# Weight and operand sums of a Strassen value projection moved to VectorE, its two half results kept apart in DRAM

## The chip, the cores and the metric

One core of one Trainium2 chip. The metric is the device time of the core for one execution of the whole program, in microseconds (us). The core has TensorE (PE in the profile, with its weight loads as PEld), VectorE (DVE), ScalarE (ACT), GpSimd (POOL) and SyncE (SP), which issues nearly all of the DMAs here.

## The reference

Two layers over x of 512 tokens by 2048 features, all in float32. The even layer comes first (sliding-window attention and a gated recurrence) and is not touched. The odd layer is the one that matters:

```python
def odd_layer(x, ln, w_in, w_out):
    h = rmsnorm(x, ln).astype(x.dtype)
    cq, ck, cv, cg = jnp.split(h @ w_in, 4, axis=-1)      # each 512 x 2048
    ...
    oc = stick_breaking_attention(heads(cq), heads(ck), heads(cv))   # 16 heads of 128
    y = (oc * jax.nn.silu(cg.astype(jnp.float32))).astype(x.dtype) @ w_out
    return x + y
```

The change concerns `cv`, the values: 512 tokens times a 2048 by 2048 weight.

## The kernel before

**Exact products.** Every float32 operand of a matmul is carried as two parts: ScalarE copies it into `hi` with rounding to fp32r (L169), VectorE takes `lo = raw - hi` (L170), and each product is three matmuls, hi·hi, lo·hi and hi·lo. Weight pieces (`raw`, 512 KB) are loaded by SP, split into `hi` and `lo` of a pool `w` with three buffers each, and taken by TensorE in a fixed order. `take()` hands out one piece and `pump()` splits up to three ahead, so VectorE can be at most about three takes ahead of TensorE. TensorE's own order is written out by hand; the other queues are ordered by a scheduler, each runs its instructions strictly in that order.

**The value projection.** The 2048 by 2048 weight is cut into four blocks of 1024 by 1024, by rows (`kh`, a half of the features) and columns (`g`, eight heads). `V_ORDER` is (g,kh) = (0,0), (1,0), (1,1), (0,1): block 0 to block 3. Each block is done by Strassen's scheme (Winograd's form) with seven products of quarters in place of eight. A product is two takes of 12 matmuls each: 2 chunks of 128 rows, 2 token halves, 3 parts. The seven products of four blocks are 672 matmuls of 128x512.

Strassen needs sums ahead of the products. *Weight sums*, function `quarter_sum`: t3 = "22"-"12" (L229), t1 = "12"-"11" (L233), t2 = t3+"11" (L237), t4 = "21"-t2 (L241), each in four pieces 128x512, so 16 per block and 64 in all, on GpSimd. The last three overwrite their inputs, so t2 has to wait until "11" has been split. `block_ahead` loads the quarters of the next block (tiles `x`, 19 buffers, and `raw`) and takes t3 and t1 early. *Operand sums*, function `operand_pair`: the two input chunks are read back from DRAM (`x1`), scaled on ScalarE (L872), and combined by four 128x256 steps: L874 and L875 on GpSimd, L876 and L877 on VectorE; then each is split. There are four pairs for each kh, made at the places in `OPERANDS_AT`.

**Results.** A product ends in two PSUM banks (128x512 each). For each result it belongs to, the first product is copied by ScalarE (L1044), a later one is added by VectorE (L1047), both marked urgent. In the kernel before, the two halves kh of a column group g go into the same tiles `halves[g]`: group 1 keeps its tiles from block 1 to block 2; group 0 is written to the DRAM tensor `vdr` after block 0, fetched again during block 2 (`fetch_half`, L1019, eight DMAs), and added into by block 3. So blocks 2 and 3 only add, by VectorE. When a group of four heads begins, SP fetches four tiles of `vdr` (L1078), which are scaled by the token norm and split (L1000, L1001).

**Around it.** Ahead of block 0 stands the even layer's output projection (L827, L850, `finish_even` at L894 to L900), with a running sum of squares on GpSimd (L407). Behind block 3 follow the 16 heads: three projections each, and the attention of the head before it, fed in between them.

Of the kernel before, what the change touches and what calls it, by code (L numbers as in the profile page):

```python
# [9 lines left out]
F32 = mybir.dt.float32  # L10
# [4 lines left out]
ALU = mybir.AluOpType  # L15
# [4 lines left out]
P = 128  # L20
D = 2048
S = 512
NC = D // P
NB = S // P
# [82 lines left out]
def trunk(ctx, tc, xt, w, lnT, lbT, gnT, qkn, sink, cs, amask, bmask, eye, cmask, out):  # L107
    nc = tc.nc
# [9 lines left out]
    dr = ctx.enter_context(tc.tile_pool(name="dr", bufs=1, space=DRAM))  # L118
    V, A, G, T = nc.vector, nc.scalar, nc.gpsimd, nc.tensor
    cnt = [0]  # L120

    def U(dt=F32, shape=(P, S)):
        cnt[0] += 1
        return u.tile(list(shape), dt, tag="u", name=f"u{cnt[0]}")
# [66 lines left out]
    for item in order:  # L191
        n = len(chunk_pieces(item))
# [29 lines left out]
    def quarter_sum(blk, name, i):  # L222

        r = quarters[blk]
        if (name, i) in r:
            return
        if name == "t3":
            r["t3", i] = X()
            G.tensor_tensor(out=r["t3", i], in0=r["22", i], in1=r["12", i], op=ALU.subtract)  # L229
        elif name == "t1":  # L230
            quarter_sum(blk, "t3", i)
            r["t1", i] = r["12", i]
            G.tensor_tensor(out=r["12", i], in0=r["12", i], in1=r["11", i], op=ALU.subtract)  # L233
        elif name == "t2":
            quarter_sum(blk, "t1", i)
            r["t2", i] = r["11", i]
            G.tensor_tensor(out=r["11", i], in0=r["t3", i], in1=r["11", i], op=ALU.add)  # L237
        else:
            quarter_sum(blk, "t2", i)
            r["t4", i] = r["21", i]  # L240
            G.tensor_tensor(out=r["21", i], in0=r["21", i], in1=r["11", i], op=ALU.subtract)  # L241

    def block_ahead(blk, m):

# [223 lines left out]
    for tt, o in ((tq, 0), (tk, 2)):  # L468
        for j in range(2):
            V.tensor_tensor(out=tt[:, j], in0=cst[:, j],  # L470
                            in1=nrm[:, o + j:o + j + 1, :].to_broadcast([P, NB, A_HD]), op=ALU.mult)
# [194 lines left out]
    for i in range(2):  # L666
        t = U(I32, [P, 4, P])
# [137 lines left out]
    for grp in range(2):  # L805
        v = evac_nat(proj_n(h, pp, 512), nat0, 512)
        for hd in range(4 * grp, 4 * grp + 4):
            f, k = forget(proj_t(h), hd)
# [58 lines left out]
    def operand_pair(kh, i):  # L867


        a, b = (sources.pop(c) for c in (8 * kh + i, 8 * kh + 4 + i))  # L870
        for t, c in ((a, 8 * kh + i), (b, 8 * kh + 4 + i)):
            A.activation(out=t, in_=t, func=AF.Copy, scale=ln[:, NC + c:NC + c + 1])  # L872
        a1, a2, b1, b2 = a[:, :256], a[:, 256:], b[:, :256], b[:, 256:]
        G.tensor_tensor(out=b2, in0=a2, in1=b2, op=ALU.add)  # L874
        G.tensor_tensor(out=a2, in0=a1, in1=a2, op=ALU.subtract)  # L875
        V.tensor_tensor(out=a1, in0=b2, in1=a1, op=ALU.subtract)  # L876
        V.tensor_tensor(out=b1, in0=b1, in1=a1, op=ALU.subtract)  # L877
        ops[kh, i] = []
        for t in (a, b):
            hi, lo = U(F32R), U(F32R)  # L880
            split(t, hi, lo)
            ops[kh, i].append((hi, lo))
# [121 lines left out]

    vdr = dr.tile([P, NB, D], F32, tag="vdr", name="vdr")
    halves = {0: {}, 1: {}}
    OPERANDS_AT = {(0, 0): ((0, 1),), (0, 1): ((0, 2), (0, 3)),
                   (1, 5): ((1, 0),), (1, 6): ((1, 1),), (2, 0): ((1, 2),), (2, 1): ((1, 3),)}  # L1010
    operand_loads(0, (2, 3))

    def fetch_half(g):

        for key in ("11", "21", "12", "22"):
            for t in range(2):
                tb, cb = t + 2 * (key[0] == "2"), 2 * g + (key[1] == "2")
                halves[g][key, t] = U()
                nc.sync.dma_start(out=halves[g][key, t], in_=vdr[:, tb, cb * S:(cb + 1) * S])  # L1019

    for blk, (g, kh) in enumerate(V_ORDER):
        res = halves[g]
        banks = {}
        for n, (name, _, pair, new, results) in enumerate(PRODUCTS[blk % 2]):
            if new:
                banks[pair] = [bank(pa if pair == 2 else pp) for _ in range(2)]
            ps = banks[pair]
            for j in range(2):
                hi, lo = take()
                for i in (2 * j, 2 * j + 1):  # L1030
                    a, b = (x[:, (i % 2) * S:(i % 2 + 1) * S] for x in (hi, lo))
                    xh, xl = block_op(kh, name, i)
                    for t in range(2):
                        k = slice(t * P, (t + 1) * P)
                        mm(ps[t], xh[:, k], a, bool(new) and not i, False)
                        mm(ps[t], xl[:, k], a, False, False)
                        mm(ps[t], xh[:, k], b, False, i == 3)
            left = [r for p in PRODUCTS[blk % 2][n + 1:] for r in p[4]]
            for t in range(2):
                for to in results:  # L1040
                    if (to, t) not in res:
                        res[to, t] = U()
                        with urgent():
                            A.activation(out=res[to, t], in_=ps[t], func=AF.Copy)  # L1044
                    else:
                        with urgent():
                            V.tensor_tensor(out=res[to, t], in0=ps[t], in1=res[to, t], op=ALU.add)  # L1047
                    if to not in left and blk != 1:
                        tb, cb = t + 2 * (to[0] == "2"), 2 * g + (to[1] == "2")
                        nc.sync.dma_start(out=vdr[:, tb, cb * S:(cb + 1) * S], in_=res[to, t])  # L1050
            if (blk, n) == (1, 4):
                operand_loads(1)
            for kh_, i in OPERANDS_AT.get((blk, n), ()):
                operand_pair(kh_, i)
            if blk == 2 and n == 4:
                fetch_half(0)

    for grp in range(4):
        for hd in range(4 * grp, 4 * grp + 4):
            ps = proj_t(h2)  # L1060
            if hd == 0:
                bc1, nat1 = token_rstd(acc2, 1)
            q = U()
            with urgent():
                V.scalar_tensor_tensor(out=q, in0=ps, scalar=float(P) ** -0.5, in1=bc1, op0=ALU.mult, op1=ALU.mult)
            q = split_u(q) + (q,)
            ps = proj_t(h2)
            k = U()
            with urgent():
                V.tensor_tensor(out=k, in0=ps, in1=bc1, op=ALU.mult)  # L1070
            k = split_u(k) + (k,)
            if hd == C_HEADS - 1:
                yy = [load_y(c) for c in range(3)]
            g = gate(proj_t(h2), bc1)
            if hd == 4 * grp:
                v = [U() for _ in range(NB)]
                for t in range(NB):
                    nc.sync.dma_start(out=v[t], in_=vdr[:, t, grp * S:(grp + 1) * S])  # L1078
                v[:3] = [split_u(x, nat1[:, t:t + 1]) for t, x in enumerate(v[:3])]
                A.activation(out=v[3], in_=v[3], func=AF.Copy, scale=nat1[:, 3:4])  # L1080
            later(attn_c(hd, q, k, g, v))
# [71 lines left out]
```

## Time and profile before

| | |
|---|---|
| time, three runs | 1840.41, 1842.22, 1842.20 us, median 1842.2 us |
| the profiled execution | 1840.83 us, of which 1839.0 us are its span |
| TensorE busy | 1806.1 us (98%), 8706 matmuls |
| VectorE busy | 1131.6 us (62%) |
| ScalarE busy | 824.5 us (45%) |
| GpSimd busy | 216.4 us (12%) |
| the value projection | from 869.6 to 1054.6 us of the span |

TensorE's busy time counts an instruction from its start to its modelled end, and the matmuls overlap, so a stretch that is fully busy need not be at its best rate; the distance between starts tells that. In a timeline the bracket behind an instruction is the idle time of its engine just before it, and what ended it. [...]

### The profile page before, as it was taken

Reading aid. Unit: us, or ns where it says so; the run is one execution under the profiler, and the core shown is the slowest. Engines: PE = TensorE matmul, PEld = TensorE weight load, DVE = VectorE, ACT = ScalarE, POOL = GpSimd, SP = SyncE. Lnnn points to the kernel's source line nnn. Section 1 sums busy time; section 2 is a strip of 40 time slices with the busy share of each in tenths; the row PEclk is TensorE's granted clock in tenths of the full one; section 3 lists DMA queues with packets and bytes.
Section 4 is the critical chain, followed back from the end, with each engine's and each line's share of the span. In section 5 each row is a group of like instructions: output and inputs, shape, how many; then the busy total and the mean of one; then the engine's idle time right before and its main releaser. Section 6 shows DMA issues by size and latency. Waiting matters only on the chain.

```text
span 1839.0 us, 22928 instructions
## 1 busy us (share of the span) xinstructions
PE 1806.1 (98%) x8706; PEld 1500.0 (82%) x8706; DVE 1131.6 (62%) x1679; ACT 824.5 (45%) x1392; POOL 216.4 (12%) x164
## 2 busy tenths in 40 slices
PE   9999999999999999999788999999999999999999
PEld 6988888888888888888666888888888888888887
DVE  7485777866556676446889845556555565556334
ACT  6455646644244453234553444445444444444211
POOL 5012211200000000126575200000000000000000
PEclk9999999999999999999999999999999999999999
DMA  6222232222222235633443332232223223235424
GB/s 231 92 82 91 81 111 84 83 87 78 75 77 85 77 125 201 208 135 138 150 144 136 121 128 91 93 113 88 95 88 111 98 83 116 90 118 173 164 80 155
DMA packets 80318, 210.32 MB, mean 114 GB/s; under 512 B 9424, under 2 KB 9936, under 8 KB 80208
## 3 DMA queue, kind: packets, MB, share of 16 engines
q1 hardware_dynamic: 77904, 204.67, 32.8%
q10 hardware_dynamic: 2304, 4.20, 0.7%
q8 instruction: 68, 1.11, 0.2%
q14 instruction: 42, 0.34, 0.1%
HBM read 185.76 MB, written 23.07 MB: 114 GB/s over the span
## 4 chain that ended last, share of the span: by engine, by line
PE 91%; DVE 3%; DMA 2%; issue 2%; POOL 1%; ACT 1%; SPq 0%; POOLq 0%; DVEq 0%; ACTq 0%
PE b L166 89%; DVE blo L170 1%; PE b L968 1%; DMA u<-in_w 1%; PE b L621 1%; DVE u L170 1%; DMA raw<-in_w 0%; DVE lo L170 0%; DMA ident<-in_eye 0%; POOL x L241 0%; DVE u L1047 0%; POOL u L407 0%; DMA u<-x 0%; DVE u L876 0%; PE b L552 0%
## 5 line engine op out<-in xcount | busy, mean ns | idle before, releaser
L166 PE MATMUL b<-u,hi 128*128 128x512 f32 x3584 | 1119.3, 393 | 0.0
L166 PEld LDWEIGHTS b<-u,hi 128*128 128x128 f32 x3584 | 663.3, 188 | 132.2
L166 PE MATMUL b<-u,lo 128*128 128x512 f32 x1792 | 698.8, 390 | 1.0 <-DVE lo L170 1.0
L169 ACT ACTIVATE hi<-raw 128x1024 fp32r<-128x1024 f32 (+2 forms) x266 | 269.9, 1015 | 652.8 <-PE b L166 599.7
L170 DVE TENSOR_TENSOR lo<-raw,hi 128x1024 fp32r<-128x1024 f32 (+2 forms) x266 | 313.0, 1177 | 224.3 <-ACT hi L169 209.1
L166 PEld LDWEIGHTS b<-u,lo 128*128 128x128 f32 x1792 | 336.3, 188 | 72.7 <-DVE lo L170 1.4
L166 PE MATMUL b<-hi,u 128*128 128x512 f32 (+1 forms) x640 | 185.1, 374 | 2.8 <-ACT u L446 1.9
L166 PE MATMUL b<-bhi,u 128*128 128x512 f32 x448 | 141.0, 396 | 0.4 <-DVE u L1047 0.4
L166 PEld LDWEIGHTS b<-hi,u 128*128 128x128 f32 x640 | 113.9, 189 | 23.5 <-ACT u L446 2.8
L166 PEld LDWEIGHTS b<-u,u 128*128 128x128 f32 (+2 forms) x928 | 115.7, 176 | 14.9 <-issue 3.5
L166 PE MATMUL b<-u,u 128*128 128x128 f32 (+5 forms) x928 | 126.7, 280 | 0.0
L166 PE MATMUL b<-lo,u 128*128 128x512 f32 (+1 forms) x320 | 118.2, 369 | 0.3 <-DVE lo L170 0.2
L166 PE MATMUL b<-blo,u 128*128 128x512 f32 x224 | 90.9, 406 | 23.0 <-DVE blo L170 22.9
L166 PEld LDWEIGHTS b<-bhi,u 128*128 128x128 f32 x448 | 85.8, 192 | 18.6 <-ACT bhi L169 0.8
L170 DVE TENSOR_TENSOR blo<-x,bhi 128x512 fp32r<-128x512 f32 x80 | 83.7, 1088 | 11.2 <-ACT bhi L169 10.9
L391 DVE TENSOR_TENSOR u<-b,bc 128x512 f32<-128x512 f32 x40 | 27.6, 689 | 79.9 <-PE b L166 79.8
L229 POOL TENSOR_TENSOR x<-x,x 128x512 f32<-128x512 f32 x16 | 24.8, 1553 | 437.4 <-ACT u L169 402.4
L166 PEld LDWEIGHTS b<-blo,u 128*128 128x128 f32 x224 | 43.0, 192 | 39.1 <-DVE blo L170 30.6
L170 DVE TENSOR_TENSOR u<-u,u 128x512 fp32r<-128x512 f32 (+1 forms) x82 | 63.9, 784 | 17.7 <-ACT u L169 17.7
L169 ACT ACTIVATE bhi<-x 128x512 fp32r<-128x512 f32 x80 | 47.2, 624 | 55.5 <-PE b L166 37.1
L166 PEld LDWEIGHTS b<-lo,u 128*128 128x128 f32 x320 | 60.3, 189 | 11.2 <-DVE lo L170 1.1
L170 DVE TENSOR_TENSOR x<-x,x 128x512 fp32r<-128x512 f32 (+2 forms) x56 | 32.4, 579 | 58.3 <-ACT x L169 58.3
(174 smaller groups left out, 1667.7 us busy)
## 6 DMA issues: line engine op xcount, KB each, us to landing
raw<-in_w SPq DMA_DIRECT2D x234, 512.0 KB, 3.2
x<-in_w SPq DMA_DIRECT2D x48, 256.0 KB, 3.1
raw<-in_w SPq DMA_DIRECT2D x24, 384.0 KB, 3.0
ydr<-x SPq DMA_DIRECT2D x32, 256.0 KB, 3.1
u<-ydr SPq DMA_DIRECT2D x32, 256.0 KB, 3.7
u<-x SPq DMA_DIRECT2D x32, 256.0 KB, 4.6
vdr<-u SPq DMA_DIRECT2D x24, 256.0 KB, 2.7
u<-vdr SPq DMA_DIRECT2D x24, 256.0 KB, 4.5
```

Source lines behind the costliest of these rows:

```text
L166: T.matmul(o, l, r, start=start, stop=stop, skip_group_check=True)
L169: A.activation(out=hi, in_=src, func=AF.Copy)
L170: V.tensor_tensor(out=lo, in0=src, in1=hi.bitcast(F32), op=ALU.subtract)
L229: G.tensor_tensor(out=r["t3", i], in0=r["22", i], in1=r["12", i], op=ALU.subtract)
L391: V.tensor_tensor(out=g, in0=ps, in1=bc, op=ALU.mult)
L621: T.transpose(out=pt[:, (2 * i + z) * P:(2 * i + z + 1) * P], in_=probs[p][b][:, z, n * P:(n + 1) * P], identity=ident)
L968: T.transpose(out=o[:, (qb - kb) * P:(qb - kb + 1) * P], in_=zs[qb][:, kb * P:(kb + 1) * P], identity=ident)
```

## The change

The 64 weight sums and the 16 first operand steps (L874, L875) are given to VectorE. The tiles that carried a half result from one block to another are gone: each block starts its own results (so ScalarE makes 32 first copies where it made 16, and VectorE 28 additions where it made 44) and writes them to one of two DRAM tensors, `vdr0` for kh 0 and `vdr1` for kh 1, 32 writes where there were 24. `fetch_half` and its eight reads are gone. When a head group begins, it fetches eight tiles in place of four, and VectorE adds them in pairs (four more 128x512 additions for each of the four groups). Everything else, TensorE's order included, is as before.

```diff
         if name == "t3":
             r["t3", i] = X()
-            G.tensor_tensor(out=r["t3", i], in0=r["22", i], in1=r["12", i], op=ALU.subtract)
+            V.tensor_tensor(out=r["t3", i], in0=r["22", i], in1=r["12", i], op=ALU.subtract)
...
-            G.tensor_tensor(out=r["12", i], in0=r["12", i], in1=r["11", i], op=ALU.subtract)
+            V.tensor_tensor(out=r["12", i], in0=r["12", i], in1=r["11", i], op=ALU.subtract)
...
-            G.tensor_tensor(out=r["11", i], in0=r["t3", i], in1=r["11", i], op=ALU.add)
+            V.tensor_tensor(out=r["11", i], in0=r["t3", i], in1=r["11", i], op=ALU.add)
...
-            G.tensor_tensor(out=r["21", i], in0=r["21", i], in1=r["11", i], op=ALU.subtract)
+            V.tensor_tensor(out=r["21", i], in0=r["21", i], in1=r["11", i], op=ALU.subtract)
...
-        G.tensor_tensor(out=b2, in0=a2, in1=b2, op=ALU.add)
-        G.tensor_tensor(out=a2, in0=a1, in1=a2, op=ALU.subtract)
+        V.tensor_tensor(out=b2, in0=a2, in1=b2, op=ALU.add)
+        V.tensor_tensor(out=a2, in0=a1, in1=a2, op=ALU.subtract)
...
-    vdr = dr.tile([P, NB, D], F32, tag="vdr", name="vdr")
-    halves = {0: {}, 1: {}}
+    vdr = [dr.tile([P, NB, D], F32, tag=f"vdr{i}", name=f"vdr{i}") for i in range(2)]
...
-        res = halves[g]
+        res = {}
...
-                    if to not in left and blk != 1:
+                    if to not in left:
...
-                        nc.sync.dma_start(out=vdr[:, tb, cb * S:(cb + 1) * S], in_=res[to, t])
+                        nc.sync.dma_start(out=vdr[kh][:, tb, cb * S:(cb + 1) * S], in_=res[to, t])
...
-            if blk == 2 and n == 4:
-                fetch_half(0)
...
-                v = [U() for _ in range(NB)]
+                v = []
                 for t in range(NB):
-                    nc.sync.dma_start(out=v[t], in_=vdr[:, t, grp * S:(grp + 1) * S])
+                    parts = U(), U()
+                    for kh in range(2):
+                        nc.sync.dma_start(out=parts[kh], in_=vdr[kh][:, t, grp * S:(grp + 1) * S])
+                    V.tensor_tensor(out=parts[0], in0=parts[0], in1=parts[1], op=ALU.add)
+                    v.append(parts[0])
```

The scheduler makes new queues of this. Three places matter, all on VectorE. In the rows, `blo<-x,bhi` is a `lo` part of a weight piece for a take, `u` are operands or results, `b` PSUM banks.

**Place 1, block 0, around the end of its second product.** Before, VectorE makes the parts of the third product's second take (blo_7452), adds the second product's banks (L1047), and finishes the operand pairs (L876, L877) that GpSimd has begun:

```order
L170 TENSOR_TENSOR blo_7452<-x_7232,bhi_7451 128x512
L170 TENSOR_TENSOR blo_7452<-x_7234,bhi_7451 128x512
L1047 TENSOR_TENSOR u_7409<-b_7427,u_7409 128x512
L1047 TENSOR_TENSOR u_7411<-b_7428,u_7411 128x512
L876 TENSOR_TENSOR u_7363<-u_7365,u_7363 128x256
L877 TENSOR_TENSOR u_7365<-u_7365,u_7363 128x256
L876 TENSOR_TENSOR u_7367<-u_7369,u_7367 128x256
L170 TENSOR_TENSOR blo_7508<-raw_7224,bhi_7507 128x1024
```

GpSimd's queue before, at the same place, from the last weight sums of block 0 (L241, t4) to the operand steps that VectorE's L876 needs:

```order
L241 TENSOR_TENSOR x_7232<-x_7232,raw_7226 128x512
L241 TENSOR_TENSOR x_7234<-x_7234,raw_7226 128x512
L229 TENSOR_TENSOR x_7597<-x_7589,x_7591 128x512
L233 TENSOR_TENSOR x_7591<-x_7591,raw_7543 128x512
L229 TENSOR_TENSOR x_7600<-x_7593,x_7595 128x512
L874 TENSOR_TENSOR u_7365<-u_7363,u_7365 128x256
L233 TENSOR_TENSOR x_7595<-x_7595,raw_7543 128x512
L875 TENSOR_TENSOR u_7363<-u_7363 128x256
```

VectorE now:

```order
L170 TENSOR_TENSOR blo_7453<-x_7232,bhi_7452 128x512
L874 TENSOR_TENSOR u_7366<-u_7364,u_7366 128x256
L1038 TENSOR_TENSOR u_7410<-b_7428,u_7410 128x512
L1038 TENSOR_TENSOR u_7412<-b_7429,u_7412 128x512
L170 TENSOR_TENSOR blo_7453<-x_7234,bhi_7452 128x512
L875 TENSOR_TENSOR u_7364<-u_7364 128x256
L874 TENSOR_TENSOR u_7370<-u_7368,u_7370 128x256
L876 TENSOR_TENSOR u_7364<-u_7366,u_7364 128x256
L875 TENSOR_TENSOR u_7368<-u_7368 128x256
L877 TENSOR_TENSOR u_7366<-u_7366,u_7364 128x256
L876 TENSOR_TENSOR u_7368<-u_7370,u_7368 128x256
L170 TENSOR_TENSOR blo_7509<-raw_7224,bhi_7508 128x1024
```

All steps of the operand pairs stand in one queue now, and the sums for the next block (L229, L233), which stood ahead of them on GpSimd, come later on VectorE.

**Place 2, block 2, its second product and the parts for the third (t4).** VectorE before, from the second product's parts to the third's (blo_8166):

```order
L170 TENSOR_TENSOR blo_8130<-x_7933,bhi_8129 128x512
L170 TENSOR_TENSOR blo_8130<-x_7935,bhi_8129 128x512
L170 TENSOR_TENSOR u_8156<-u_7965,u_8155 128x512
L1047 TENSOR_TENSOR u_7783<-b_8109,u_7783 128x512
L1047 TENSOR_TENSOR u_7785<-b_8110,u_7785 128x512
L170 TENSOR_TENSOR u_8160<-u_7967,u_8159 128x512
L170 TENSOR_TENSOR blo_8166<-x_7911,bhi_8165 128x512
L170 TENSOR_TENSOR blo_8166<-x_7913,bhi_8165 128x512
```

VectorE now, the last twelve rows up to the first half of the same parts (blo_8177):

```order
L237 TENSOR_TENSOR raw_7870<-x_7988,raw_7870 128x512
L875 TENSOR_TENSOR u_7970<-u_7970 128x256
L241 TENSOR_TENSOR x_7914<-x_7914,raw_7870 128x512
L876 TENSOR_TENSOR u_7970<-u_7972,u_7970 128x256
L237 TENSOR_TENSOR raw_7870<-x_7991,raw_7870 128x512
L877 TENSOR_TENSOR u_7972<-u_7972,u_7970 128x256
L170 TENSOR_TENSOR u_8167<-u_7970,u_8166 128x512
L241 TENSOR_TENSOR x_7916<-x_7916,raw_7870 128x512
L1038 TENSOR_TENSOR u_8156<-b_8174,u_8156 128x512
L1038 TENSOR_TENSOR u_8158<-b_8175,u_8158 128x512
L170 TENSOR_TENSOR u_8171<-u_7972,u_8170 128x512
L170 TENSOR_TENSOR blo_8177<-x_7914,bhi_8176 128x512
```

Weight sums t2 and t4 and whole operand pairs now stand in VectorE's queue ahead of the parts that TensorE takes next.

**Place 3, the first head group.** VectorE before, from the gate of head 0 (L391) on:

```order
L391 TENSOR_TENSOR u_8981<-b_8920,bc_8822 128x512
L170 TENSOR_TENSOR lo_9015<-raw_9012,hi_9014 128x1024
L396 SCALAR_TENSOR_TENSOR u_8983<-u_8981,u_8983 128x512
L398 TENSOR_TENSOR u_8981<-u_8981,u_8983 128x512
L1001 SCALAR_TENSOR_TENSOR u_8999<-u_8990,nat_8823,u_8998 128x512
L947 SCALAR_TENSOR_TENSOR x_9046<-b_9024,x_9046 128x512
```

VectorE now:

```order
L391 TENSOR_TENSOR u_8990<-b_8929,bc_8831 128x512
L170 TENSOR_TENSOR lo_9036<-raw_9033,hi_9035 128x1024
L396 SCALAR_TENSOR_TENSOR u_8992<-u_8990,u_8992 128x512
L1070 TENSOR_TENSOR u_8999<-u_8999,u_9000 128x512
L398 TENSOR_TENSOR u_8990<-u_8990,u_8992 128x512
L947 SCALAR_TENSOR_TENSOR x_9067<-b_9045,x_9067 128x512
L1070 TENSOR_TENSOR u_9004<-u_9004,u_9005 128x512
```

The four additions L1070 wait for two DMAs each, and stand among the rows of the attention and ahead of the next `lo`.

## Rows read from the trace of the kernel before

**Rows 1.** Stretches of the span: PE, PEld, DVE, ACT, POOL busy us (instructions), clock, DMA share, GB/s.
```profile
740.00:860.00 120.00, 120.00 (x531) 99.41 (x530) 57.46 (x62) 40.78 (x54) 33.36 (x20) 1.00 0.48 168
860.00:900.00 40.00, 30.39 (x122) 22.86 (x121) 33.95 (x35) 21.63 (x37) 30.00 (x23) 0.94 0.26 89
900.00:940.00 40.00, 40.00 (x172) 32.93 (x172) 31.74 (x35) 21.64 (x37) 18.33 (x12) 0.97 0.48 159
940.00:1000.00 60.00, 46.20 (x183) 34.24 (x182) 54.85 (x57) 27.05 (x44) 40.78 (x29) 0.97 0.39 134
1000.00:1060.00 60.00, 60.00 (x266) 49.72 (x265) 50.18 (x59) 23.61 (x35) 19.43 (x12) 1.00 0.45 151
1060.00:1600.00 540.00, 540.00 (x2552) 450.32 (x2552) 298.68 (x395) 253.38 (x400) 0.00 (x0) 1.00 0.29 99
```

**Rows 2.** TensorE's waits, 860 to 1060: total us, times, longest.
```profile
PE b L166 <- DVE blo L170: 22.9, 13, 5.4
```

**Rows 3.** TensorE's timeline: start, us, what; block 0's start, longest stall, steady rate, end.
```profile
869.55 0.61 PE L166 MATMUL b<-bhi,u 128*128 128x512 f32 x2
...
897.88 0.79 PE L166 MATMUL b<-blo,u 128*128 128x512 f32 x1 [5.38 <-DVE blo L170]
...
905.11 0.62 PE L166 MATMUL b<-bhi,u 128*128 128x512 f32 x2
...
905.79 0.62 PE L166 MATMUL b<-bhi,u 128*128 128x512 f32 x2
...
1054.37 0.39 PE L166 MATMUL b<-blo,u 128*128 128x512 f32 x1
```

**Rows 4.** TensorE alone, short stretches: us, busy (instructions), clock, DMA share, GB/s.
```profile
898.00:902.00 4.00, 4.00 (x10) 0.50 0.65 213
...
994.00:998.00 4.00, 4.00 (x12) 0.57 0.88 290
```

**Rows 5.** Timeline: four GpSimd sums in a row, and VectorE beside them.
```profile
969.10 7.05 POOL L237 TENSOR_TENSOR raw<-x,raw 128x512 f32<-128x512 f32 x4 [3.63 <-DVE blo L170]
...
971.52 1.78 DVE L170 TENSOR_TENSOR blo<-x,bhi 128x512 fp32r<-128x512 f32 x1
973.22 1.78 DVE L170 TENSOR_TENSOR u<-u,u 128x512 fp32r<-128x512 f32 x1
```

**Rows 6.** Timeline of VectorE while GpSimd stands still.
```profile
868.42 0.43 DVE L876 TENSOR_TENSOR u<-u,u 128x256 f32<-128x256 f32 x1 [2.69 <-POOL u L875]
868.88 0.42 DVE L877 TENSOR_TENSOR u<-u,u 128x256 f32<-128x256 f32 x1
...
884.89 0.68 DVE L170 TENSOR_TENSOR blo<-x,bhi 128x512 fp32r<-128x512 f32 x1
885.49 0.68 DVE L170 TENSOR_TENSOR u<-u,u 128x512 fp32r<-128x512 f32 x1
...
898.35 0.41 DVE L877 TENSOR_TENSOR u<-u,u 128x256 f32<-128x256 f32 x1
898.68 1.21 DVE L170 TENSOR_TENSOR blo<-raw,bhi 128x1024 fp32r<-128x1024 f32 x1
899.82 0.68 DVE L170 TENSOR_TENSOR u<-u,u 128x512 fp32r<-128x512 f32 x1
```

**Rows 7.** GpSimd's first sums (t3), 740 to 1060: count, busy us, mean ns, idle before, releasers.
```profile
L229 POOL TENSOR_TENSOR x<-x,x 128x512 f32<-128x512 f32 x16 | 24.8, 1553 | 437.4 <-ACT u L169 402.4 <-DMA x<-in_w 22.5 <-DVE blo L170 12.4
```

**Rows 8.** VectorE, block 0: the wait for an operand step of GpSimd.
```profile
894.56 0.93 DVE L876 TENSOR_TENSOR u<-u,u 128x256 f32<-128x256 f32 x1 [2.58 <-POOL u L875]
```

**Rows 9.** GpSimd's timeline: a sum that waits for its load.
```profile
1000.86 1.29 POOL L229 TENSOR_TENSOR x<-x,x 128x512 f32<-128x512 f32 x1 [8.67 <-DMA x<-in_w]
```

**Rows 10.** The head group's fetch: SP's issue, VectorE behind it, time to landing.
```profile
1086.36 2.06 SPq L1078 DMA_DIRECT2D u<-vdr  x4
...
1098.60 1.22 DVE L170 TENSOR_TENSOR lo<-raw,hi 128x1024 fp32r<-128x1024 f32 x1
...
DMA to landing us min/median/max: 3.7/4.5/4.9
```

More of the change, by code (lines that the diff above doesn't have):

```diff
@@ L1011, in trunk @@
     operand_loads(0, (2, 3))
[L1013 to L1019, printed above, removed]
     for blk, (g, kh) in enumerate(V_ORDER):
-        res = halves[g]
+        res = {}
         banks = {}
```

## The prediction

> **What bounds the kernel now.** I read the stretches first, then TensorE's waits, then its timeline. TensorE is busy without a gap from 740 to 860 and from 1060 to 1600, but only 30.4 of 40 us from 860 to 900 and 46.2 of 60 from 940 to 1000, 23.4 us idle in all [rows 1]. Both stretches lie in the value projection, and 22.9 us of it, in 13 waits, end with a `lo` part from VectorE [rows 2]. VectorE is busy 34.0 and 54.9 us there, ScalarE only 21.6 and 27.1 [rows 1]. So inside this stage VectorE is the limit, and everywhere else TensorE.
>
> How much is there to win? Block 0 starts at 869.55; the last matmul starts at 1054.37, and one slot of 0.23 later the stage is over, at 1054.60 [rows 3]: 185.0 us. At the steady rate three matmuls take 0.68 us (905.11 to 905.79 [rows 3]), so 672 take 152.3. [...]
>
> Why is VectorE full? Beside a row of GpSimd sums its 128x512 steps start 1.70 us apart (971.52, 973.22), one for each sum of 7.05/4 = 1.76 us [rows 5]. With GpSimd still they start 0.60 apart (884.89, 885.49); a 128x256 step takes 0.33 and a 128x1024 step 1.14 [rows 6]. So a GpSimd sum that meets VectorE costs it 1.1 us, and the same sum on VectorE costs 0.6.
>
> **The change part by part.**
>
> *Sums.* 64 weight sums at 0.60 are 38.4 us, 16 operand steps at 0.33 are 5.3. Without them VectorE needs, at unhindered prices, 80 `lo` parts of 0.60, 16 of 1.14, 28 additions of 0.60 (were 44), and for operands 16 steps of 0.33 and 16 splits of 0.60: 48.0 + 18.2 + 16.8 + 5.3 + 9.6 = 97.9. Together 141.6 us, of which about 7 (t3 and t1 of block 0, an operand pair) fall ahead of the stage, where VectorE has over 60 of 120 us free [rows 1]. So some 135 us stand against 152 of TensorE; before, VectorE was busy 170.7 us from 860 to 1060 [rows 1]. On average it fits. But VectorE may run only three takes (8.2 us) ahead, so I walk the new queue through the two places that stalled; a product lasts 5.44 us.
>
> *Block 0 (place 1).* From the end of the output projection, when product 0 begins, the new queue has 16 steps of 0.60, one of 0.33 and two casts (0.2 us each, an estimate: 128 columns, where 256 take 0.33) up to the second product's additions: 10.3 us, and the banks are ready at 10.9. Behind that: 1.2 for the additions, 0.6, six steps of 0.33 and the 1.14 of blo_7509: done at 16.0. Its first user, the third matmul of product 3, comes at 16.3 + 0.45. No stall, by 0.7 us. The 2.58 us wait of L876 for GpSimd [rows 8] and the 5.4 us stall behind it go. The two last squares (L407) still run on GpSimd and can cost 1.1 each: stall 0 to 3, taken 1.
>
> *Block 2 (place 2).* VectorE last waits for TensorE at the additions for product 5 of block 1. From there to the first half of blo_8177 stand 22 steps of 0.60, ten of 0.33 and two of 1.14: 18.8 us, started 0.2 after the banks. TensorE has three products until then, 16.3 + 0.45. So it waits 2.2. The next part stands behind four weight sums: 0.6 + 2.4 + 0.33 + 0.6 = 3.9 against a take of 2.7, 1.2 more; the one after, 0.33 + 1.14 + 0.6 against half a take, 0.7 more. A step that follows the one whose result it reads costs more, 0.46 after L876 where 0.33 is usual (868.42, 868.88 [rows 6]); nine such make 1. Sum 5, bounds 3 to 8. Then block 2 asks 11.4 us for three products of 16.3, and block 3, of the same kind as block 1, 31 us for 38: no stall.
>
> *Clock.* A 5 us sum of short stalls may or may not bring the lower level again; 0 to 2, taken 1. Other resumptions 1.
>
> *Results.* First copies on ScalarE: 16 more at the 0.6 us that VectorE's cost; it is busy under 24 of 60 us from 1000 on [rows 1]. SP loses eight reads and gains eight writes; nothing.
>
> *Head groups (place 3).* Eight fetches at 2.06/4 = 0.52 us each start at 1086.36, so the last lands at 1086.4 + 4.1 + 4.5 = 1095.0 [rows 10]; by the queue the fourth addition stands near 1098. The weight load behind moves 2 us later. The next `lo` part, at 1098.60 before [rows 10], comes 2.4 us (four additions) later; TensorE had no wait in this part [rows 1]. Cost 0; if that cover were gone, up to 2.4 a group, 10 in all. I take 0: 540 of 540 us busy says that the cover is wide.
>
> **Sum:** 32.7 - 1 - 5 - 1 - 1 = 24.7 won, bounds 32.7 - 3 = 29.7 (only block 2's least stall) and 32.7 - 3 - 8 - 2 - 2 = 17.7. The profiled execution took 1840.8; it becomes 1816.1. The median of the runs is 1.4 above it: 1842.2 - 24.7 = 1817.5, rounded **1818**, its own range 1812 to 1825.
>
> **The rivals.**
>
> *A: VectorE's steps keep a higher price, and VectorE stays the limit.* A recorded step lasts 0.68 [rows 6], though the next starts after 0.60. If in the new queue, where many steps wait for a predecessor or for ScalarE's `hi`, each costs 0.69 (and 0.41, 1.21), block 2's stretch is 15.2 + 4.1 + 2.4 = 21.7, 5.1 late, the next two 1.8 and 1.0; with the 1 for dependent steps about 9. Block 0 loses its 0.7 of cover and 2 more, say 3 with the squares, the clock 2, resumptions 1: 15 lost, 17.7 won: about 1825; and if each take also waits on the chain sum, `hi`, `lo`, up to 1834. I put it at 1827. For it: long runs of dependent steps in place 2. Against: the 0.60 was read in steps whose inputs came just in time.
> [...]
>
> *B: slower, because loads now hold up VectorE.* L229 waits for two loads. On GpSimd such waits were 22.5 us in all [rows 7], 8.67 at the longest [rows 9], and harmless; now `lo` parts stand behind them. The loads wait in SP's queue behind writes of results, which wait for VectorE's additions, so a late VectorE makes its own loads late. If blocks 1, 2 and 3 each lose 8.67 and 2.1 of lower clock, that is 32.3: 1817.5 + 32.3 = 1850. It decides once the loss is over 8.2 us a block, which eats the 24.7. Against: the eight reads that stood between those loads are gone, and in my walk each load is issued some 8 us ahead of its sum.
>
> *C: the change doesn't do what it says.* TensorE then waits as long for ScalarE's `hi` (which needs the sums too) as it did for `lo`: within 3 us of 1842. Against: ScalarE is a little over half busy [rows 1].
>
> **How the numbers follow.** Forecast 0.66 (1812 to 1825), A 0.17 (1825 to 1834), below 1812, where also block 2 hardly stalls, 0.05, B 0.08, C 0.04. Faster by over 0.2% (3.7 us, about what a measurement of this kernel can tell from no change): 0.66 + 0.17 + 0.05 = 0.88; same 0.04; slower 0.08. Eight in ten: I leave out B, C and the upper end of A: 1809, where nothing is lost (1842.2 - 32.7), to 1832.
>
> **What would show it.** Right: GpSimd without L229 to L241; VectorE's 128x512 steps near 0.60 apart all through the stage; from block 0's start to the last matmul of block 3 about 160 us in place of 185; no TensorE wait near block 0's start over 1.5 us; a few waits for `blo`, 5 us in all, around the third product of block 2, some 90 us behind block 0's start; PEclk 1.0 in nearly all of it; no idle TensorE behind 1060. Wrong: VectorE idle before L229 on a load (B); TensorE waiting for `bhi` (C); steps 0.7 apart (A); waits of TensorE at the head groups, four times, which would mean that the fetch is not hidden.

## The result

The changed kernel takes 1815.72 us (median of four runs, 1814.91 to 1816.32) against 1842.11 us beside it: a ratio of 0.9859, 95% interval 0.9841 to 0.9876. It is faster by 26.4 us, and inside the predicted range.

The profiled execution took 1816.32 us, its span is 1814.5 us. The first view is the stretches of the span, as in [rows 1]: us, then the busy time (instructions) of PE, PEld, DVE, ACT and POOL, granted clock (PEclk, a share of TensorE's full speed), DMA share, GB/s.

```profile
860.00:900.00 40.00, 38.78 (x171) 31.74 (x171) 39.77 (x67) 29.48 (x50) 7.53 (x3) 1.00 0.41 136
900.00:940.00 40.00, 40.00 (x178) 33.13 (x177) 32.62 (x50) 24.07 (x39) 0.00 (x0) 1.00 0.64 213
940.00:1000.00 60.00, 56.54 (x240) 45.56 (x238) 56.88 (x94) 33.43 (x55) 0.00 (x0) 0.97 0.43 147
1000.00:1035.00 35.00, 35.00 (x156) 28.99 (x155) 21.68 (x31) 16.41 (x26) 0.00 (x0) 1.00 0.37 126
1035.00:1575.00 540.00, 540.00 (x2552) 450.38 (x2551) 307.02 (x410) 253.04 (x400) 0.00 (x0) 1.00 0.32 107
```

TensorE lost 9.6 and 13.8 us of idle time in the first and third stretch of before [rows 1]; it loses 1.2 and 3.5 now. GpSimd does nothing behind 900. VectorE is fuller than before (39.8 of 40, 56.9 of 60) and yet TensorE waits less: a 128x512 step of VectorE beside GpSimd's sums took 1.70 us of that time [rows 5], and it takes 0.60 now.

TensorE's timeline, in the form of [rows 3]: the start of block 0, all waits of the stage (in the brackets), and the last matmul.

```profile
870.48 0.62 PE L166 MATMUL b<-bhi,u 128*128 128x512 f32 x2
...
888.63 0.50 PE L166 MATMUL b<-blo,u 128*128 128x512 f32 x1 [1.22 <-DVE blo L170]
...
948.97 0.50 PE L166 MATMUL b<-blo,u 128*128 128x512 f32 x1 [0.17 <-DVE blo L170]
...
963.45 0.50 PE L166 MATMUL b<-blo,u 128*128 128x512 f32 x1 [3.26 <-DVE blo L170]
...
1030.15 0.39 PE L166 MATMUL b<-blo,u 128*128 128x512 f32 x1
```

The stage runs from 870.48 to 1030.15 + 0.23: **159.9 us in place of 185.0**, 25.1 less. It starts 0.9 later than before, and behind it stand 784.1 us where 784.4 stood. So all of the gain is in the value projection, and the head groups pay nothing for their extra fetch. The 13 waits of [rows 2] are three, and TensorE's granted clock fell only once, behind the longest of them, to 0.57 in the mean of a 4 us stretch (TensorE alone: us, busy, granted clock, DMA share, GB/s; [rows 4] has two such stretches):

```profile
964.00:968.00 4.00, 4.00 (x12) 0.57 0.18 66
968.00:972.00 4.00, 3.97 (x18) 1.00 0.43 141
```

Twelve matmuls stand where 17.6 would fit at the steady rate of three in 0.68 us, a loss of some 1.3 us.

VectorE's costliest groups in and just ahead of the stage (860 to 1035; busy us, mean ns of one, idle time before and its releaser), and below them the additions of the head groups (860 to 1600):

```profile
L170 DVE TENSOR_TENSOR blo<-x,bhi 128x512 fp32r<-128x512 f32 x80 | 53.2, 691 | 11.1 <-ACT bhi L169 10.5
L229 DVE TENSOR_TENSOR x<-x,x 128x512 f32<-128x512 f32 x12 | 8.1, 682 | 0.0
...
L1070 DVE TENSOR_TENSOR u<-u,u 128x512 f32<-128x512 f32 x16 | 11.0, 684 | 0.0
```

No sum L229 waits for a load (on GpSimd those waits were 22.5 us [rows 7]), and no addition of a head group waits for its DMAs.

### The profile page after: what moved, and what is told of

It reads as the page before. It is cut to its first block, busy times and chain, and to the rows that moved or that the text cites. A ratio compares the mean times of both kernels' runs of the same rounds, so it can differ in the third digit from the quotient of the medians.

```text
span 1814.5 us, 22940 instructions
## 1 busy us (share of the span) xinstructions
PE 1801.1 (99%) x8706; PEld 1500.9 (83%) x8706; DVE 1125.2 (62%) x1759; ACT 833.0 (46%) x1408; POOL 102.5 (6%) x84
## 4 chain that ended last, share of the span: by engine, by line
PE 49%; DVE 2%; issue 0%; DMA 0%; ACT 0%
PE b L166 48%; PE b L968 1%; DVE blo L170 1%; DVE u L170 0%; DVE u L1038 0%; DVE x L241 0%; DMA vdr<-u 0%; ACT bhi L169 0%; DVE u L899 0%; DVE u L876 0%; DVE u L877 0%; DVE u L875 0%; DVE u L874 0%; DVE raw L237 0%; DVE x L229 0%
## 5 line engine op out<-in xcount | busy, mean ns | idle before, releaser
L407 POOL TENSOR_TENSOR u<-u,u 128x512 f32<-128x512 f32 x30 | 51.4, 1713 | 522.3 <-ACT u L406 521.7
L391 DVE TENSOR_TENSOR u<-b,bc 128x512 f32<-128x512 f32 x40 | 27.6, 689 | 79.9 <-PE b L166 79.7
L170 DVE TENSOR_TENSOR u<-u,u 128x512 fp32r<-128x512 f32 (+1 forms) x82 | 55.5, 679 | 17.5 <-ACT u L169 17.5
L166 PE MATMUL b<-x,u 128*128 128x128 f32 (+3 forms) x360 | 65.3, 327 | 0.0
L169 ACT ACTIVATE u<-u 128x512 fp32r<-128x512 f32 (+1 forms) x82 | 50.5, 618 | 29.9 <-DMA u<-ydr 22.0
```

The source lines that it names most:

```text
L166: T.matmul(o, l, r, start=start, stop=stop, skip_group_check=True)
L169: A.activation(out=hi, in_=src, func=AF.Copy)
L170: V.tensor_tensor(out=lo, in0=src, in1=hi.bitcast(F32), op=ALU.subtract)
L391: V.tensor_tensor(out=g, in0=ps, in1=bc, op=ALU.mult)
L407: G.tensor_tensor(out=acc, in0=acc, in1=s, op=ALU.add)
```

## The experiments

Each is the changed kernel with one edit, except where said. Every time below is a median; what stands in brackets behind it is the ratio to the kernel before, run beside it on the same chip, with its 95% interval.

**1. The sums alone, and 2. the halves alone.** The change has two parts, so each was run without the other. Experiment 1 keeps `vdr`, `halves` and `fetch_half` of the kernel before, and takes all sums on VectorE; experiment 2 keeps the sums on GpSimd, and the halves apart. Their edits, from the changed kernel (of the first, the core):

```diff
-    vdr = [dr.tile([P, NB, D], F32, tag=f"vdr{i}", name=f"vdr{i}") for i in range(2)]
+    vdr = dr.tile([P, NB, D], F32, tag="vdr", name="vdr")
+    halves = {0: {}, 1: {}}
...
-        res = {}
+        res = halves[g]
...
+            if blk == 2 and n == 4:
+                fetch_half(0)
```

```diff
-            V.tensor_tensor(out=r["t3", i], in0=r["22", i], in1=r["12", i], op=ALU.subtract)
+            G.tensor_tensor(out=r["t3", i], in0=r["22", i], in1=r["12", i], op=ALU.subtract)
...
-        V.tensor_tensor(out=b2, in0=a2, in1=b2, op=ALU.add)
-        V.tensor_tensor(out=a2, in0=a1, in1=a2, op=ALU.subtract)
+        G.tensor_tensor(out=b2, in0=a2, in1=b2, op=ALU.add)
+        G.tensor_tensor(out=a2, in0=a1, in1=a2, op=ALU.subtract)
```

> Of the two parts only the first: all sums on VectorE, the half results still carried in tiles and added by VectorE, fetched back as before. Theory (GpSimd's sums beside VectorE's two-input steps are what made the stage late): most of the 26 us stays won, but VectorE has 16 more additions (9.6 us) in blocks 2 and 3, two of them ahead of the late parts of block 2, so 1816 to 1824 us. Rival (the carried halves were the bottleneck): 1838 to 1842 us.

> Of the two parts only the second: each block starts its own results, two tensors in DRAM, added at the head groups; all sums still on GpSimd. Theory: VectorE loses 9.6 us of additions in blocks 2 and 3, but every GpSimd sum beside a VectorE step still costs it 1.1 us, so TensorE still waits in block 0 and in block 2: 1832 to 1842 us. Rival (the carried halves were the bottleneck): 1816 to 1822 us.

The sums alone give 1816.68 us (0.9866, 0.985 to 0.9882), the halves alone 1840.88 (0.9997, 0.9988 to 1.0007). TensorE's waits between 860 and 1060 (total us, times, longest), of the sums alone and then of the halves alone:

```profile
PE b L166 <- DVE blo L170: 5.4, 3, 3.4
```

```profile
PE b L166 <- DVE blo L170: 20.6, 14, 5.4
```

The move of the sums is the whole change, as far as these runs can tell: the value projection takes 161.1 us with the sums alone and 159.9 with the whole change, and the intervals of the two ratios overlap. Taking 16 additions of 0.6 us off VectorE, which is what the halves do in blocks 2 and 3, changes nothing measurable alone: the 5.39 us stall of block 0 remains, and it stands where no addition was saved.

**3. GpSimd back beside VectorE.** Was GpSimd harmful because VectorE *waited* for its sums, or because the two engines slow each other? Here every weight sum stays on VectorE, and behind each GpSimd makes one more step that reads the sum and writes a tile that nobody uses. Nothing in the kernel needs its results.

```diff
+    def beside(x):
+        G.tensor_tensor(out=wz, in0=x, in1=x, op=ALU.add)
...
             V.tensor_tensor(out=r["t3", i], in0=r["22", i], in1=r["12", i], op=ALU.subtract)
+            beside(r["t3", i])
```

> The changed kernel, and behind each of the 64 weight sums GpSimd reads the sum and writes an unused tile (one tensor_tensor of 128x512, both inputs in SBUF). Nothing waits for these except the release of the sum's tile. Theory (GpSimd's mere running slows VectorE): each of the 64 that meets VectorE costs it up to 1.1 us, VectorE's work in the stage goes from 135 to as much as 205 us against TensorE's 152, so 1840 to 1870 us. Rival (what hurt was that results came late from a slow engine, a matter of dependence only): 1815 to 1820 us.

1842.38 us (1.0007, 0.9998 to 1.0017): all of the gain is gone. VectorE's parts and GpSimd's extra steps, 860 to 1060 (lines moved by four):

```profile
L170 DVE TENSOR_TENSOR blo<-x,bhi 128x512 fp32r<-128x512 f32 x80 | 71.5, 924 | 3.8 <-ACT bhi L169 3.6
```

```profile
L224 POOL TENSOR_TENSOR wz<-x 128x512 bf16<-128x512 f32 x42 | 68.6, 1633 | 61.7 <-DVE x L233 30.6 <-DVE x L248 27.3 <-DVE x L238 2.1
```

A part takes 924 ns where it took 691, and VectorE waits for GpSimd nowhere in this trace. So two engines that run side by side are enough to cost this much; no dependence is needed. That the time is just that of the kernel before is chance, since VectorE still makes its own sums here. What GpSimd's sums cost VectorE in the kernel before shows when the whole value projection of that kernel is set beside that of experiment 1 (columns as in the first view):

```profile
869.55:1054.60 185.05, 161.65 (x673) 127.36 (x672) 162.45 (x174) 89.10 (x145) 100.75 (x68) 0.97 0.40 135
```

```profile
870.16:1031.22 161.06, 155.67 (x674) 126.77 (x672) 147.48 (x237) 87.21 (x141) 3.91 (x2) 0.99 0.46 154
```

With the sums taken over, VectorE makes 237 steps in place of 174 and is busy 15 us less.

**4. GpSimd busy, but not reading.** The same place, with a copy of one column (so that it starts at the same time) and two fills in place of the step that reads:

```diff
+    def beside(x):
+        G.tensor_copy(out=wz[:, 0:1], in_=x[:, 0:1])
+        G.memset(wz, 0.0)
+        G.memset(wz, 0.0)
```

> The changed kernel, and behind each of the 64 weight sums GpSimd copies one column of the sum and then fills an unused 128x512 tile twice, which reads nothing. Theory (GpSimd slows VectorE's two-input steps by its reads of SBUF): VectorE's 128x512 steps stay 0.60 us apart, 1815 to 1820 us. Rival (any running GpSimd instruction slows VectorE): 128x512 steps of 1.2 to 1.7 us beside the fills, 1835 us or more.

1822.96 us (0.99, 0.9886 to 0.9915), some 7 us more than the changed kernel and 3 outside what was expected. The parts are not slower, and the fills take 525 ns each:

```profile
L170 DVE TENSOR_TENSOR blo<-x,bhi 128x512 fp32r<-128x512 f32 x80 | 52.7, 686 | 10.0 <-ACT bhi L169 9.6
```

```profile
L226 POOL MEMSET wz<- 128x512 bf16 x58 | 30.5, 525 | 3.3
```

GpSimd's timeline and VectorE's show where a part of the 7 us comes from (start, us):

```profile
884.72 10.17 POOL L224 CAST wz<-x 128x1 bf16<-128x1 f32 x1
```

```profile
897.76 0.69 DVE L235 TENSOR_TENSOR x<-x,x 128x512 f32<-128x512 f32 x1 [2.92 <-POOL wz L224]
```

The copy of one column lasted 10.17 us, where the mean of such copies is 0.70, and ended, at 894.89, 0.04 us behind a run of VectorE's steps that kept their usual distances (884.73 to 894.85). The sum's tile stayed taken, and VectorE's next t3 (L235 here) waited 2.92 us for it. There are two such waits, 5.1 us in all, and VectorE's t3 waits 4.8 us more for loads, which it does nowhere in the changed kernel. The first are of the experiment's own making; how the 7 us divide between them was not traced further. The reading of the pair stands all the same: beside GpSimd's steps that read, a part takes 924 ns, and beside its fills 686.

**5. One more step on VectorE.** How much room has VectorE now? The extra step of experiment 3, but on VectorE:

```diff
+    def beside(x):
+        V.tensor_tensor(out=wz, in0=x, in1=x, op=ALU.add)
```

> The changed kernel, and behind each of the 64 weight sums VectorE itself does one more 128x512 step of the same kind on an unused tile (38.4 us in all). Theory (VectorE has now 135 us of work in a stage of 152 to 160, so 17 to 25 us to spare): some 56 of the 64 fall into the stage, 34 us, and 135 + 34 = 169 is 9 us over the stage, more with the waits that it cannot fill: 1826 to 1838 us, less than the 1842 that the same steps on GpSimd gave. Rival (VectorE still has ample room): 1816 to 1820 us.

1843.95 us (1.0015, 1.0006 to 1.0024). This missed. 56 of the 64 steps fall into the value projection, 33.6 us at 0.60, and make it 27.4 us longer (187.3): VectorE took in only some 6 us, not 17 or more. By its mean load it would have room for more, since TensorE needs 152.3 us and the steps as walked 135. Most of its idle time in the changed kernel are waits of its parts for ScalarE's `bhi`, 16.4 us in 18 pieces (waits, 860 to 1040; total, times, longest):

```profile
DVE blo L170 <- ACT bhi L169: 16.4, 18, 1.5
```

These pieces can hold work: with the sums alone (experiment 1) VectorE makes 15 additions more in the stage, its waits for `bhi` fall to 9.5 us, and the stage is only 1.2 us longer. But nearly all of them lie in blocks 1 and 3 (916 to 938 and 998 to 1023), where TensorE waits for nothing, and the extra steps stand beside the weight sums, of which only ten of 54 lie there. So the place of a step seems to decide what it costs; no run tried this by itself. With the extra steps TensorE's waits lie all over the stage, and ScalarE's parts are among them (860 to 1060):

```profile
PE b L166 <- DVE blo L170: 17.2, 10, 2.8
...
PE b L166 <- ACT bhi L169: 4.8, 2, 3.1
```

These waits are 17.3 us more than the changed kernel's 4.7. A part of the other 10.1 goes with TensorE's lower clock (0.95 in the mean of the stage, 0.99 in the changed kernel); how they divide was not traced further.

Set beside experiment 3: a step that reads beside VectorE costs the kernel 26.7 us, and the same number of steps *on* VectorE 28.2. Within the noise (the intervals overlap), such a step on GpSimd is no cheaper for the kernel than one on VectorE.

**6. The first operand steps back on GpSimd** (L874 and L875 of all eight pairs, nothing else).

```diff
-        V.tensor_tensor(out=b2, in0=a2, in1=b2, op=ALU.add)
-        V.tensor_tensor(out=a2, in0=a1, in1=a2, op=ALU.subtract)
+        G.tensor_tensor(out=b2, in0=a2, in1=b2, op=ALU.add)
+        G.tensor_tensor(out=a2, in0=a1, in1=a2, op=ALU.subtract)
```

> The changed kernel with only the 16 operand steps (L874, L875, 128x256) back on GpSimd; the 64 weight sums stay on VectorE. Theory (the 5.4 us stall of block 0 came from VectorE's L876 waiting for these steps in GpSimd's queue, behind weight sums): without the weight sums ahead of them GpSimd is free, but its steps meet VectorE's stream; VectorE waits some 1 to 3 us at L876 in block 0 and perhaps in block 2, so 1816 to 1821 us. Rival (the operand steps carry most of the gain): 1825 us or more.

1820.32 us (0.9886, 0.9869 to 0.9902): as expected, and 4.6 worse than the change. VectorE waits for GpSimd again, and TensorE behind it, in block 0 (the last two lines are of the waits, 860 to 1040):

```profile
891.57 0.50 PE L166 MATMUL b<-blo,u 128*128 128x512 f32 x1 [4.62 <-DVE blo L170]
...
PE b L166 <- DVE blo L170: 7.5, 5, 4.6
...
DVE u L876 <- POOL u L875: 2.8, 3, 1.5
```

No weight sum stands ahead of GpSimd's operand steps here, but a square (L407) does, and beside VectorE's steps it lasted 9.69 us:

```profile
875.91 9.69 POOL L407 TENSOR_TENSOR u<-u,u 128x512 f32<-128x512 f32 x1 [4.38 <-ACT u L406]
```

The operand steps begin behind its end, at 885.57. So these 16 small steps, undone alone, cost 4.6 us, by a wait of the kind of [rows 8]. What is left, most of the gain, is the 64 weight sums'.

**7. Earlier operands.** The 3.26 us wait of block 2 stands behind whole operand pairs in VectorE's queue (place 2). Taking these pairs three products earlier, in block 1, might free it:

```diff
-                   (1, 5): ((1, 0),), (1, 6): ((1, 1),), (2, 0): ((1, 2),), (2, 1): ((1, 3),)}
+                   (1, 2): ((1, 0),), (1, 3): ((1, 1),), (1, 4): ((1, 2),), (1, 5): ((1, 3),)}
...
-            if (blk, n) == (1, 4):
+            if (blk, n) == (1, 1):
```

> The changed kernel with the operand pairs of kh 1 (and their loads) made three products earlier, in block 1, where VectorE waits for ScalarE and TensorE. Theory (what is left, 3.3 us of wait in block 2, the lower clock of 4 us behind it and the resumption, comes from operand pairs and weight sums standing together ahead of the parts for t4): most of it goes, 1810 to 1813 us. Rival (block 1 has no room either, or the operands' loads come late): 1815 us or more.

1816.23 us (0.9864, 0.9849 to 0.9878): that theory fell. The wait only moved to the turn of block 1:

```profile
947.70 0.50 PE L166 MATMUL b<-blo,u 128*128 128x512 f32 x1 [2.49 <-DVE blo L170]
```

The same edit on the kernel of experiment 1 did the same:

> The same earlier operand pairs, in the kernel that has only the sums moved and still carries its half results in tiles (as the run with sums alone, 1816.7 us). Theory: the same gain, 1811 to 1814 us; the carried tiles leave fewer free buffers in block 1 and VectorE has 16 more additions, so up to 2 us slower than the other. Rival: the buffers are missing and the loads come late, 1817 us or more.

1817.19 us (0.9868, 0.9853 to 0.9883), with a wait of 2.48 us at 946.50. In both, the pairs only push other parts back. VectorE still waits 5.2 us for `bhi` from 916 to 926 of the first of these traces, ahead of the pairs; whether work can be brought there was not tried.

**8. The best of both?** Experiment 6 hurt in block 0 and left block 2 with shorter waits. So the first operand steps were given to GpSimd for kh 1 alone, and then, in addition, the last three squares (L407) to VectorE. The changed kernel was run again beside them.

```diff
-        V.tensor_tensor(out=b2, in0=a2, in1=b2, op=ALU.add)
-        V.tensor_tensor(out=a2, in0=a1, in1=a2, op=ALU.subtract)
+        E = G if kh else V
+        E.tensor_tensor(out=b2, in0=a2, in1=b2, op=ALU.add)
+        E.tensor_tensor(out=a2, in0=a1, in1=a2, op=ALU.subtract)
```

```diff
-            G.tensor_tensor(out=acc, in0=acc, in1=s, op=ALU.add)
+            (eng or G).tensor_tensor(out=acc, in0=acc, in1=s, op=ALU.add)
...
-        add_square(acc2, t, n == 0)
+        add_square(acc2, t, n == 0, V if n > 12 else G)
```

> The changed kernel once more, on the same chip as the next two, so that two versions can be set against it: 1815 to 1817 us, with TensorE waits of some 4.7 us in the stage, 1.2 of them at the start of block 0 and 3.3 ahead of the third product of block 2, and a lower granted clock for some 4 us behind the second.

> The changed kernel, but the first two operand steps (L874, L875) of the pairs of kh 1 go back to GpSimd; those of kh 0 (block 0) stay on VectorE. Theory (from the experiment that gave all of them back): the steps on GpSimd hurt block 0, where VectorE waits for them, and help block 2, where VectorE is ten steps of 0.33 us late; then block 0 waits 1.2 us as in the changed kernel, block 2 some 2.9 us in short pieces instead of 3.3 in one, without the lower clock behind it: 1 to 3 us less than the changed kernel, 1812.5 to 1815. Rival: GpSimd's steps beside VectorE's give back what VectorE saves, as everywhere else: 1815 to 1818.

> The one before, and in addition the last three running squares of the output projection (L407) on VectorE, so that no GpSimd operation runs beside the start of block 0. Theory: the 1.2 us wait of block 0 comes from VectorE's steps of 1.78 us beside those squares, and goes: another 0.5 to 1.2 us, 1811.5 to 1814. Rival: three more steps of 0.6 us on VectorE make up for it, and the time is that of the one before within 0.5 us.

1815.73 us (0.9859, 0.9844 to 0.9873), 1815.53 (0.9859, 0.9844 to 0.9873) and 1815.79 (0.9861, 0.9844 to 0.9877): no difference, and the rivals hold. With the steps split, block 2's wait comes in four short pieces, as expected, but the whole stage is 159.3 us against 159.5 of the changed kernel beside it:

```profile
949.58 0.50 PE L166 MATMUL b<-blo,u 128*128 128x512 f32 x1 [0.74 <-DVE blo L170]
952.25 0.50 PE L166 MATMUL b<-blo,u 128*128 128x512 f32 x1 [1.02 <-DVE blo L170]
965.23 0.50 PE L166 MATMUL b<-blo,u 128*128 128x512 f32 x1 [0.44 <-DVE blo L170]
967.97 0.50 PE L166 MATMUL b<-blo,u 128*128 128x512 f32 x1 [0.66 <-DVE blo L170]
```

With the squares on VectorE too, no GpSimd step is left near block 0, and still there is a wait, of 1.50 us:

```profile
888.51 0.51 PE L166 MATMUL b<-blo,u 128*128 128x512 f32 x1 [1.50 <-DVE blo L170]
```

Three more steps of 0.6, 1.8 us, stand against the 1.6 that the squares beside VectorE had cost it (below). The lower clock that was expected for the changed kernel did not come in its second profile (below too). No version here beats the change.

## Why the prediction was right, step by step

**The stage.** Predicted some 160 us, measured 159.9. The 32.7 us that the sum starts from are 185.0 - 152.3. That it is so close is partly luck: the losses were taken as 1 us in block 0, 5 in block 2, 1 for the clock and 1 for resumptions, 8 in all, and came out as 1.2, 3.4, 1.3 and a rest of 1.7, 7.6 in all, so that a block 2 taken 1.6 too high pays for the other three. The profiled execution was to take 1816.1 us and took 1816.32. The miss on the median, 1818 against 1815.72, is almost wholly the last step of the working: the profiled run of before lay 1.4 us under its median, that of after 0.6 over it.

**VectorE's price.** Back to back, the steps start 0.60 apart through the whole stage, and 0.33 for 128x256, with recorded durations of 691 ns and 418; beside the squares at block 0's start two distances are longer (below). So rival A is out: the 0.69 that it took as the price of a step is the recorded duration, and the next step starts some 0.09 us before its end.

**Block 0.** Predicted 0 to 3, taken 1, for the squares; measured 1.22, and the squares are only part of it. VectorE's timeline around the end of the output projection, and GpSimd's:

```profile
871.71 0.68 DVE L850 TENSOR_TENSOR u<-b,u 128x512 f32<-128x512 f32 x1
872.31 1.79 DVE L170 TENSOR_TENSOR blo<-x,bhi 128x512 fp32r<-128x512 f32 x2
874.02 1.78 DVE L899 SCALAR_TENSOR_TENSOR u<-u,ln,u 128x512 fp32r<-128x512 f32 x1
875.73 0.68 DVE L241 TENSOR_TENSOR x<-x,raw 128x512 f32<-128x512 f32 x1
...
883.56 1.27 DVE L1038 TENSOR_TENSOR u<-b,u 128x512 f32<-128x512 f32 x2
```

```profile
868.34 4.61 POOL L407 TENSOR_TENSOR u<-u,u 128x512 f32<-128x512 f32 x1 [3.65 <-ACT u L406]
873.81 1.44 POOL L407 TENSOR_TENSOR u<-u,u 128x512 f32<-128x512 f32 x1 [0.86 <-ACT u L406]
```

From 872.31 to 875.73 VectorE needs 3.4 us for three steps, 1.6 more than three times 0.60: the two squares. The additions L1038 start 13.1 us after block 0, where the walk had 10.3: 1.6 for the squares and 1.2 because 18 steps stood ahead of them, not 16. The rest of the walk (5 us from the additions to the first half of blo_7509) held. The 5.4 us stall went with the wait of [rows 8].

**Block 2.** Predicted 5 in three pieces (2.2 + 1.2 + 0.7, and 1 for dependent steps), bounds 3 to 8; measured 3.26, with 0.17 ahead of it, at the place that was named (the third product, 93 us behind block 0's start). The size is right, the parts are not. The stretch from the additions at 944.36 to the end of the first half of blo_8177 took 18.95 us, 18.8 by the walk. The 1 us for dependent steps was wrong. The 0.46 of [rows 6] stands between a step and the very next one that reads its result; in the new queue another step stands between the two every time, and of the ten 128x256 steps nine have the usual distance and one 0.44 (959.26 to 959.70):

```profile
952.44 0.43 DVE L875 TENSOR_TENSOR u<-u 128x256 f32<-128x256 f32 x1
952.77 0.69 DVE L170 TENSOR_TENSOR blo<-x,bhi 128x512 fp32r<-128x512 f32 x1
953.38 0.43 DVE L876 TENSOR_TENSOR u<-u,u 128x256 f32<-128x256 f32 x1
...
959.26 0.43 DVE L877 TENSOR_TENSOR u<-u,u 128x256 f32<-128x256 f32 x1
959.70 0.69 DVE L170 TENSOR_TENSOR u<-u,u 128x512 fp32r<-128x512 f32 x1
```

The rows of the queue at place 2 had shown that already. In its place VectorE came some 1.2 us late into the stretch: TensorE begins block 2 at 948.19, so the banks of the product before last were ready one product (5.44) earlier, near 942.8 to 943.0, and the additions start at 944.36 instead of 0.2 behind that. VectorE, then ScalarE, ahead of it:

```profile
937.56 1.29 DVE L170 TENSOR_TENSOR blo<-x,bhi 128x512 fp32r<-128x512 f32 x2 [1.18 <-ACT bhi L169]
...
944.36 1.28 DVE L1038 TENSOR_TENSOR u<-b,u 128x512 f32<-128x512 f32 x2
```

```profile
935.01 2.00 ACT L872 ACTIVATE u<-u,ln 128x512 f32<-128x512 f32 x3 [0.96 <-DMA u<-x]
936.91 1.14 ACT L169 ACTIVATE bhi<-x 128x512 fp32r<-128x512 f32 x2
```

VectorE waited 1.18 us for `bhi`, which stood in ScalarE's queue behind the scalings L872, which waited for their read-back. A walk of VectorE's queue alone can't see that. So two errors in this term, 1 us too much and 1.2 too little, nearly cancel. The second and third pieces did not show in this execution, whose next take ran at the lower clock (0.57) and so gave VectorE 1.3 us more. In the second profile of the changed kernel the clock stayed at 1.00, and there they are, 0.59 and 0.40 (predicted 1.2 and 0.7), the first now ended by ScalarE's `bhi`, which waits for the same weight sums:

```profile
963.40 0.50 PE L166 MATMUL b<-blo,u 128*128 128x512 f32 x1 [3.30 <-DVE blo L170]
966.55 0.73 PE L166 MATMUL b<-bhi,u 128*128 128x512 f32 x2 [0.59 <-ACT bhi L169]
969.42 0.50 PE L166 MATMUL b<-blo,u 128*128 128x512 f32 x1 [0.40 <-DVE blo L170]
```

**Clock and resumptions.** Taken 1 and 1; measured 1.3 (above) and a rest of 1.7, which is 159.9 - 152.3 less 4.65 of waits and 1.3. No run shows 1 us of resumptions by itself: behind each of the three waits the next matmul starts 0.34 us after the first where 0.23 is usual, 0.1 us more, and what makes up the remainder was not traced. The second profile leaves 1.7 too, without the lower clock (159.5 - 152.3 - 5.5 of waits). In the kernel before, the two stretches of [rows 4] had lost 1.7 and 1.3 us, counted in the same way; the first slow spell as a whole, ten matmuls from 897.88 to 902.31, took 4.43 us for 2.27, 2.2 lost, near the 2.1 that rival B took for a block. So between the two executions of the changed kernel the lower clock cost the stage only 0.4 us, 159.9 against 159.5: what it took it mostly gave back as waits that did not come.

**Head groups, B and C.** Cost 0, as taken: 540 of 540 us busy behind 1035. No L229 waits for a load in the stage, and TensorE waits for no `bhi` (0.59 us in the second profile). The "halves" part, whose reads stood between the loads before, was not needed for that: experiment 1 keeps those reads, and its value projection is only 1.2 us longer.

**Where the reason needs correction.** The argument priced a GpSimd sum that meets VectorE at 1.1 us of VectorE's time and the same sum on VectorE at 0.6. Experiment 3 shows a smaller price on the average: VectorE's recorded busy time in the stage rose from 139.95 us (870 to 1030) to 179.56 (871 to 1056), 39.6 for 55 steps, 0.7 each; steps of GpSimd beside which VectorE's kept their 0.60 us, or that met an addition from PSUM (679 ns; last section), are among them. Nor is VectorE's average load (135 of 152) a margin that can be spent anywhere: experiment 5 found some 6 us. The time that was forecast did not rest on that average but on the walk through two places, and these were the places that waited.

## What to carry to other kernels

A second engine that worked beside the one that is the limit was not free here: 64 steps of GpSimd that nobody needed cost 26.7 us (experiment 3). Price such help by what the limiting engine's own steps last while it runs, and compare this with the price of doing the work there. Walk the limiting engine's queue through the places that stall, with distances between starts rather than durations, and follow the queue of each engine that feeds it as well; a mean load under 100% (135 of 152 us here) said little about the room at the place where a step would stand (some 6 us, experiment 5). Leaving the sums to GpSimd to relieve a full VectorE costs this kernel 24 us (experiment 1 against before).

## What the runs showed of the hardware

Some GpSimd steps beside VectorE's lasted far longer than others of their kind. GpSimd's steps and VectorE's took turns in the trace of before, one for one, 1.76 and 1.70 us each [rows 5]. In experiment 3, where the mean of its kind is 1.63, this step of GpSimd lasted 9.79 us:

```profile
904.77 9.79 POOL L224 TENSOR_TENSOR wz<-x 128x512 bf16<-128x512 f32 x1 [12.26 <-DVE x L233]
```

All the while VectorE's steps started 0.60 us apart as if alone, some 16 of them. In experiment 4 a copy of 128 by 1 took 10.17 us beside steps as close. What VectorE did when the 9.79 us ended shows in its row:

```profile
913.58 2.47 DVE L1046 TENSOR_TENSOR u<-b,u 128x512 f32<-128x512 f32 x4
```

These are its first steps in that stretch that read a PSUM bank and so one tile of SBUF, not two; GpSimd's step is through 0.98 us behind the start of the first. The additions are not slowed either: in this trace they last 679 ns in the mean, where a `blo` part lasts 924. The changed kernel shows the same: its square of 4.61 us (L407 at 868.34, shown above) ends 1.24 us behind the start of L850, VectorE's only PSUM reader there. In experiment 4 the copy ended 0.04 us behind the end of VectorE's run. So of these three long steps two ended 0.98 and 1.24 us behind the start of a VectorE step that reads PSUM, and one at a pause of VectorE. No run varied this by itself, so what kept these steps long was not shown, nor what decides at the outset between turns and a long step.
